# Sixteen experts streamed through one ring of tiles: large and small experts taken by turns

## The chip, the cores and the metric

The kernel runs on one core of one Trainium2 chip. The metric is the device time in microseconds (us) of one execution. Three executions of the kernel before took 1281.28, 1287.78 and 1290.25 us; the median is 1287.78 us.

## The reference: one layer, and most of its bytes are expert weights

The layer has 256 tokens of width 2048 in fp32. A gated short convolution comes first (a projection to 3 x 2048, a depthwise convolution over three tokens, a projection back), modulated by six vectors that come from a conditioning vector times a 2048 x 12288 matrix, then a LayerNorm. The second half is a mixture of 16 experts with top-1 of 4 groups and top-2 of the 4 experts in the group:

```
act = silu(h @ w_gate[e]) * (h @ w_up[e])          # 2048 -> 768, for every expert e
y   = sum over e of (act * combine[:, e]) @ w_down[e]   # 768 -> 2048
x   = layer_norm(ALPHA * x + mod[5] * y)
```

`combine` is zero but for a token's two experts. An expert's weights are 3 x 2048 x 768 x 4 bytes, 18.9 MB, whatever the number of its tokens; the sixteen make 302 MB of the 472 MB that the kernel reads.

## The kernel before, in words

**Ranks and slots.** The kernel counts the tokens of each expert on the chip, sorts the experts by count and calls them by rank. Each rank has a fixed number of slots, `CAPS` (L42): rank 0 is handled apart with 32, ranks 1 to 3 have 128 slots, ranks 4 to 6 have 64, ranks 7 to 15 have 32. A rank with 128 slots is called a large expert here, one with 32 a small one. (What exceeds the slots is done in a loop at the end, L1336, that runs as often as there is excess.)

**The weights.** `expert_loads` (L144) lists 12 tiles of 1.5 MiB for an expert: gate and up weights in turn for four quarters of the 2048 input rows (`q`, four blocks of 128 rows each), then four tiles of down weights. All weights of the kernel go through one list, `loads`, in one order. `get(i)` (L118) asks for tile i, and before it returns it issues the following loads, on SP's queue (SyncE), as far as the ring has room. The ring has `RING = 6` buffers; a load can start when the tile six places earlier in the list has been read for the last time.

**One expert.** `gather` (L892) makes the expert's input in transposed form with one-hot matmuls on TensorE (tiles `gap`), and ScalarE and VectorE modulate it. `run_expert` (L1019) then goes through the quarters. A small expert multiplies its 32 columns with 384-wide pieces of the weights (`gue`, L1049, 128x32 weights in TensorE). A large expert uses 128x128; half of its row blocks go as fp32 (L1049), the others are split on ScalarE (L795) and VectorE (L796) into a high and a low part (`parts`, three pairs of buffers) and multiplied three times (L1045 to L1047). Then come the activation, its transposes (`pte`, L1071) and `down_rows` (L978), which goes through the four down tiles (`dne`; L1007 for a small expert, L1010 to L1012 for a large one). Halfway, at down tile 1, `mid` may call `prepare`, the gather for a later group of experts (`GROUPS`, `PREPARE`, L45). `down_rows` returns a function `finish`, which scales the result (`Y`, L1155) and, for a large expert (`Alone`, L1112) or for the last of a pack of four small ones (`Packed`, L1131), scatters it back to the 256 tokens (`sce`, L1125 and L1163, then an addition into `acc`). It is called after the first quarter of the next expert (`before`, L1051).

**The order of the work.** `SEQ` (L43) gives the ranks in turn, one after the other. Inside this, the framework's own planner sets each engine's order of instructions: it puts work that does not depend on the current expert (the gather, the residual sums `lr`) between its matmuls. Accumulators in PSUM come from six banks (`mm`) and two more (`aux`).

Of the kernel before, what the change touches and what calls it, by code (L numbers as in the profile page):

```python
# [36 lines left out]
AT = 1  # L37
# [28 lines left out]
def trunk_kernel(  # L66
# [77 lines left out]
    def expert_loads(e, pieces=None):  # L144
# [4 lines left out]
        for q in range(4):  # L149
            for src in (ex_w_gate, ex_w_up):  # L150
                def fn(w, src=src, q=q):
                    s = one(src)[:, q * 512 : (q + 1) * 512, :]
                    nc.sync.dma_start(w, s.rearrange("o (p j) f -> p (o j f)", j=4))
                gu.append(add_load(fn))
        if pieces is None:
            for i in range(4):
                def fn(w, hf=i // 2, c0=i % 2 * 3072):
                    s = one(ex_w_down)[:, hf * 384 : hf * 384 + 384, :]
                    nc.sync.dma_start(w, s.rearrange("o (p j) f -> p (o j f)", j=3)[:, c0 : c0 + 3072])
                dn.append(add_load(fn))  # L160
            return gu, dn
        for c0, n in pieces:
            def fn(w, c0=c0, n=n):
                for hf in range(2):
# [4 lines left out]
                    )  # L169
            dn.append((add_load(fn), c0, n))  # L170
        return gu, dn


# [538 lines left out]
    ld_exp = {0: expert_loads(0)}  # L712
    wide["free"] = todo[max(i for i, st in enumerate(steps) if st in last_cin)][0]
# [63 lines left out]
    with tc.tile_pool(name="p2", bufs=1) as p2:  # L777
# [200 lines left out]
        def down_rows(dn, a, al, cc, name, out, mid, at, pieces):  # L978
# [9 lines left out]
            for i, ld in enumerate(dn):  # L988
# [4 lines left out]
                for j, lo_c, hi_c, w0 in rows_:  # L993
                    kt = i // 2 * 3 + j
                    for (c0, n), (bank, off) in zip(pieces, where):
                        f = n // k
                        for g in range(k):
# [20 lines left out]

        def run_expert(lds, xs, cc, name, out, between=(), mid=None, at=0, before=None, pieces=None):  # L1019

# [7 lines left out]
            for q in range(4):  # L1028
                wg, wu = get(gu[2 * q]), get(gu[2 * q + 1])
                for k in range(4):  # L1030
# [3 lines left out]
                    for g in range(4 if cc == 32 else 2):  # L1034
                        for hf in range(1 if cc == 32 else 2):
# [48 lines left out]
            if isinstance(dn[0], int):  # L1084
                return down_rows(dn, a, al if cc == 128 else None, cc, name, out, mid, at, pieces)

# [13 lines left out]
            for i, (ld, c0, n) in enumerate(dn):  # L1100
# [3 lines left out]
                if prev:  # L1104
                    out(*prev)
                prev = (ps, c0, n)
            out(*prev)

        def m5_cols(p0, pn, c0, n):
# [188 lines left out]
        prepare(0)  # L1298
        for r in SEQ[1:]:
            ld_exp[r] = expert_loads(expert_id(r), PIECES if r == SEQ[-1] else None)  # L1300
        done = None
        for r in SEQ:
            if r == SEQ[1]:
                prepare(1)
# [7 lines left out]
            done = run_expert(ld_exp[r], xgs[r], CAPS[r], f"e{r}_", out_r, extra, mid, AT, done,  # L1312
                              PIECES if SEQ[-1] in pack_of.get(r, ()) else None)


# [20 lines left out]
        with tc.For_i(0, nov, 1) as it:  # L1336
# [12 lines left out]
            for h in range(2):  # L1349
# [3 lines left out]
                V.tensor_sub(op_[:, h, :], op_[:, h, :], oc_)  # L1353
            lds = expert_loads(eo)
            xg = gather([(op_, 128)], "ov")
            run_expert(lds, xg, 128, "ov", Alone(op_, ow_, "ov", then=stats2))()
            finish()
# [27 lines left out]
```

## Time and profile before

| | |
|---|---|
| median of three runs | 1287.78 us |
| the profiled execution: its own time, its span | 1292.59 us, 1290.9 us |
| TensorE (PE) busy | 1130.1 us, 88% of the span |
| VectorE (DVE), ScalarE (ACT) busy | 677.3 us (52%), 376.0 us (29%) |
| moved by DMA | 475.60 MB, mean 368 GB/s over the span |
| chain that ended last | PE 62%, DMA 23%, DVE 9%, ACT 2%, issue 2% |

The page also cuts the span into 40 slices of 32.3 us. The experts fill the slices from the 17th on; the rate of the DMA in them reads 340 425 429 429 405 343 322 422 429 406 361 377 428 430 423 337 428 428 429 429 429 429 414 82 GB/s. The busy share of TensorE alone does not say which of the two, matmuls or transfers, ends a stage: a matmul that overlaps others counts as busy, and a transfer that has no free buffer is not waiting by any count.

### The profile page before, as it was taken

Reading aid. Unit: us, or ns where it says so; the run is one execution under the profiler, and the core shown is the slowest. Engines: PE = TensorE matmul, PEld = TensorE weight load, DVE = VectorE, ACT = ScalarE, POOL = GpSimd, SP = SyncE. Lnnn points to the kernel's source line nnn. Section 1 sums busy time; section 2 is a strip of 40 time slices with the busy share of each in tenths; the row PEclk is TensorE's granted clock in tenths of the full one; section 3 lists DMA queues with packets and bytes.
Section 4 is the critical chain, followed back from the end, with each engine's and each line's share of the span. In section 5 each row is a group of like instructions: output and inputs, shape, how many; then the busy total and the mean of one; then the engine's idle time right before and its main releaser. Section 6 shows DMA issues by size and latency. Waiting matters only on the chain.

```text
span 1290.9 us, 19457 instructions
## 1 busy us (share of the span) xinstructions
PE 1130.1 (88%) x7743; PEld 755.7 (59%) x7743; DVE 677.3 (52%) x1273; ACT 376.0 (29%) x662; POOL 9.7 (1%) x50
## 2 busy tenths in 40 slices
PE   4999779999999998976789997999689998789984
PEld 2867659877999964533257543664157443444453
DVE  1456549897999967352255542573146441123127
ACT  1532333533444424140035312451026110100020
POOL 1000000000000000000000000000000000000000
PEclk9999799999999999699889999999899999899996
DMA  9999898689999977899998899999999899999992
GB/s 317 395 400 395 303 382 297 225 312 398 360 334 343 333 280 291 340 425 429 429 405 343 322 422 429 406 361 377 428 430 423 337 428 428 429 429 429 429 414 82
DMA packets 151105, 475.60 MB, mean 368 GB/s; under 512 B 11000, under 2 KB 70104, under 8 KB 126688
## 3 DMA queue, kind: packets, MB, share of 16 engines
q1 hardware_dynamic: 145984, 471.89, 92.6%
q10 hardware_dynamic: 5024, 2.40, 0.7%
q8 instruction: 63, 1.03, 0.3%
q14 instruction: 34, 0.28, 0.1%
HBM read 472.16 MB, written 2.10 MB: 367 GB/s over the span
## 4 chain that ended last, share of the span: by engine, by line
PE 62%; DMA 23%; DVE 9%; ACT 2%; issue 2%; SPq 0%; DVEq 0%; ACTq 0%
DMA w<-in_ex_w_up_dram 19%; PE ci L464 18%; PE gue L1049 14%; PE co L597 6%; DMA w<-in_ex_w_gate_dram 4%; PE dne L1007 3%; PE gap L921 3%; PE gv L269 3%; PE sce L1163 2%; PE gv L299 2%; PE gue L1047 1%; PE dne L1010 1%; PE dne L1011 1%; PE dne L1012 1%; PE gue L1046 1%
## 5 line engine op out<-in xcount | busy, mean ns | idle before, releaser
L1049 PE MATMUL gue<-w,xgp 128*32 128x384 f32 (+1 forms) x1664 | 216.7, 536 | 65.3 <-DMA w<-in_ex_w_up_dram 58.0
L464 PE MATMUL ci<-hhi,hic 128*128 128x256 f32 x768 | 193.2, 289 | 9.0 <-ACT hic L418 7.9
L1049 PEld LDWEIGHTS gue<-w,xgp 128*32 128x32 f32 (+1 forms) x1664 | 80.3, 124 | 197.9 <-issue 88.7
L464 PE MATMUL ci<-hlo,hic 128*128 128x256 f32 x768 | 190.0, 285 | 0.1
L464 PEld LDWEIGHTS ci<-hhi,hic 128*128 128x128 f32 x768 | 148.4, 193 | 18.3 <-ACT hic L418 12.2
L464 PEld LDWEIGHTS ci<-hlo,hic 128*128 128x128 f32 x768 | 148.4, 193 | 0.7 <-DVE hlo L413 0.4
L419 DVE TENSOR_TENSOR loc<-w,hic 128x1024 fp32r<-128x1024 f32 (+1 forms) x108 | 118.5, 1103 | 44.3 <-PE ci L464 22.7
L418 ACT CAST hic<-w 128x1024 fp32r<-128x1024 f32 (+1 forms) x108 | 102.4, 957 | 118.5 <-PE ci L464 71.7
L796 DVE TENSOR_TENSOR parts<-w,parts 128x384 fp32r<-128x384 f32 (+1 forms) x168 | 97.8, 613 | 57.3 <-ACT parts L795 55.3
L464 PE MATMUL ci<-hhi,loc 128*128 128x256 f32 x768 | 110.2, 285 | 7.4 <-DVE loc L419 7.4
L795 ACT CAST parts<-w 128x384 fp32r<-128x384 f32 (+1 forms) x168 | 89.9, 560 | 79.4 <-PE gue L1046 59.9
L464 PEld LDWEIGHTS ci<-hhi,loc 128*128 128x128 f32 x768 | 99.3, 191 | 13.6 <-DVE loc L419 7.6
L1068 ACT COPY gse<-gue 128x384 f32<-128x384 f32 x16 | 7.6, 480 | 313.9 <-PE gue L1049 313.9
L277 DVE SCALAR_TENSOR_TENSOR rows<-w,sT,rows 128x512 f32<-128x512 f32 x105 | 78.2, 749 | 3.6 <-ACT rows L273 2.0
L921 PEld LDWEIGHTS gap<-ohp,xt 128*128 128x128 f32 x512 | 66.2, 209 | 22.6 <-issue 16.0
L921 PE MATMUL gap<-ohp,xt 128*128 128x128 f32 (+2 forms) x512 | 70.4, 294 | 5.7 <-DVE xgp L889 5.0
L1049 PE MATMUL gue<-w,xfp 128*128 128x384 f32 x192 | 71.5, 495 | 1.7 <-DMA w<-in_ex_w_gate_dram 1.7
L1155 DVE TENSOR_TENSOR Y<-dne,m 32x512 f32<-32x512 f32 (+3 forms) x84 | 40.6, 484 | 37.9 <-PE dne L1007 34.6
L889 DVE TENSOR_SCALAR xgp<-gap,GB 128x32 f32<-128x32 f32 (+1 forms) x104 | 31.6, 314 | 48.6 <-ACT xgp L887 48.0
L597 PE MATMUL co<-hio,yh 128*128 128x512 f32 x128 | 52.1, 407 | 1.9 <-DVE t L607 1.4
L887 ACT ACTIVATE xgp<-gap,GB 128x32 f32<-128x32 f32 (+1 forms) x104 | 37.9, 385 | 52.3 <-PE gap L921 29.9
L418 ACT CAST hio<-w 128x1024 fp32r<-128x1024 f32 x32 | 33.2, 1049 | 60.5 <-PE co L597 25.1
(316 smaller groups left out, 1415.4 us busy)
## 6 DMA issues: line engine op xcount, KB each, us to landing
w<-in_ex_w_gate_dram SPq DMA_DIRECT2D x64, 1536.0 KB, 14.6
w<-in_ex_w_up_dram SPq DMA_DIRECT2D x64, 1536.0 KB, 17.1
w<-in_ex_w_down_dram SPq DMA_DIRECT2D x60, 1536.0 KB, 14.0
w<-in_mod_w_dram SPq DMA_DIRECT2D x48, 1536.0 KB, 8.4
w<-in_conv_in_w_dram SPq DMA_DIRECT2D x84, 512.0 KB, 8.3
w<-in_mod_w_dram SPq DMA_DIRECT2D x22, 1024.0 KB, 8.3
w<-in_conv_out_w_dram SPq DMA_DIRECT2D x16, 1024.0 KB, 8.9
w<-in_conv_in_w_dram SPq DMA_DIRECT2D x24, 256.0 KB, 7.2
```

The lines of the kernel that those rows point to most:

```text
L269: TE.matmul(box["ps"][32 * g : 32 * g + 32, :n], sT[:, kt : kt + 1].to_broadcast([P, 32]), ws, start=kt < 4, stop=kt >= 12)
L277: V.scalar_tensor_tensor(out=box["r"][:, :n], in0=ws, scalar=sT[:, kt : kt + 1], in1=box["r"][:, :n], op0=ALU.mult, op1=ALU.add)
L418: S.copy(hi[:, :n], src)
L419: V.tensor_sub(lo[:, :n], src, hi[:, :n].bitcast(F32))
L464: TE.matmul(pss[a][:, b * T : (b + 1) * T], w_[:, o : o + P], h_[:, k0 + k, :], start=first and not low and (b, k, i) == (0, 0, 0), stop=l ...
L597: TE.matmul(pso[h][:, :], y[:, k, h * P : (h + 1) * P], w_[:, k * 512 : (k + 1) * 512], start=not low and (qt % 2, pr, k, i) == (0, 0, 0, ...
L795: S.copy(hi[:, :n], src)
L796: V.tensor_sub(lo[:, :n], src, hi[:, :n].bitcast(F32))
L921: TE.matmul(ps[:, k * n : (k + 1) * n], xn[:, h, (k0 + k) * P : (k0 + k + 1) * P], oh[:, h, :n], start=h == 0, stop=h == 1)
L1007: TE.matmul(ps, a[kt], ws, start=st_, stop=sp_)
L1049: TE.matmul(dst, big[0][:, KF.index(kt), :] if cc == 128 else xg[:, kt, :cc], src, start=st_, stop=sp_)
L1155: V.tensor_tensor(out=y, in0=ps[p0 : p0 + cc, :f], in1=m5_cols(p0, cc, c, f), op=ALU.mult)
```

## The change

The ranks are put into `UNITS`: either one rank, or a large rank with a small one ([1, 14], [2, 12], [3, 10]). `SEQ` is the units one after the other, so each large expert comes one place earlier in it, and its small partner behind it. `queue_loads` enters the loads of a unit into the list by turns: the gate and up tile of a quarter for the first expert, then those of the second, and so on, then the down tiles one of each. `run_expert` and `down_rows` become generators that yield after each quarter and each down tile; `by_turns` steps the generators of a unit in turn and, after the first step, calls what the last unit left (`finish`). `PREPARE` moves the gather of rank 1 from expert 14 to expert 15; the overflow list and the residual sums (`lr`) move from the third to the second expert in `SEQ`, which is 15. No tile, matmul, size or buffer count changes.

```diff
-SEQ = [0, 15, 14, 1, 13, 12, 2, 11, 10, 3, 9, 4, 8, 5, 6, 7]
+UNITS = [[0], [15], [1, 14], [13], [2, 12], [11], [3, 10], [9], [4], [8], [5], [6], [7]]
+SEQ = [r for unit in UNITS for r in unit]
...
-PREPARE = {14: 2, 13: 3, 12: 4, 11: 5, 9: 6, 8: 7}
+PREPARE = {15: 2, 13: 3, 12: 4, 11: 5, 9: 6, 8: 7}
...
+    def queue_loads(fns):
...
+        out = [([], []) for _ in fns]
+        for q in range(4):
+            for (gu, _), (g, _) in zip(fns, out):
+                g += [add(fn) for fn in gu[2 * q : 2 * q + 2]]
+        for i in range(max(len(dn) for _, dn in fns)):
+            for (_, dn), (_, d) in zip(fns, out):
+                d += [add(fn) for fn in dn[i : i + 1]]
+        return out
...
-                if q == 0 and before:
-                    before()
+                yield
...
+        def by_turns(gens, before=()):
+
+            left, live = [], list(gens)
+            while live:
+                for gen in live[:]:
+                    try:
+                        next(gen)
+                    except StopIteration as e:
+                        live.remove(gen)
+                        if e.value:
+                            left.append((-gens.index(gen), e.value))
+                    for fn in before:
+                        fn()
+                    before = ()
+            return [fn for _, fn in sorted(left, key=lambda t: t[0])]
...
-            extra = {SEQ[0]: [sum_m5], SEQ[2]: [overflow_list, residual], SEQ[-1]: [last_rows]}.get(r, [])
+            extra = {SEQ[0]: [sum_m5], SEQ[1]: [overflow_list, residual], SEQ[-1]: [last_rows]}.get(r, [])
...
+        left = []
+        for unit in UNITS:
+            if unit == UNITS[1]:
+                prepare(1)
+            left = by_turns([expert(r) for r in unit], left)
```

Three places show how this moves instructions. The line numbers of the changed kernel are higher by 16 or so.

The first is TensorE's queue at the end of the first quarter of rank 1 (128x384 results are the large expert's, 32x384 a small one's; `w_` is the weight tile that is read). Before:

```order
2324 L1047 MATMUL gue_2_5845<-parts,xhp_5733 128x384
2325 L1045 MATMUL gue_3_5846<-parts,xhp_5733 128x384
2326 L1046 MATMUL gue_3_5846<-parts,xlp_5734 128x384
2327 L1047 MATMUL gue_3_5846<-parts_4884,xhp_5733 128x384
2328 L1049 MATMUL gue_0_5843<-w_5811,xfp_5732 128x384
2329 L1049 MATMUL gue_1_5844<-w_5811,xfp_5732 128x384
```

Now:

```order
2289 L1064 MATMUL gue_3_5717<-parts_4884,xhp_5604 128x384
2290 L1066 MATMUL gue_0_5774<-w_5682,xgp_5322 32x384 x2
2291 L1066 MATMUL gue_0_5774<-w_5690,xgp_5322 32x384 x2
...
2296 L1066 MATMUL gue_0_5774<-w_5682,xgp_5322 32x384 x2
2297 L1066 MATMUL gue_0_5774<-w_5690,xgp_5322 32x384 x2
2298 L1066 MATMUL gue_0_5714<-w_5698,xfp_5603 128x384
2299 L1066 MATMUL gue_1_5715<-w_5698,xfp_5603 128x384
```

A quarter of rank 14, eight rows on its own two tiles, now stands between two quarters of rank 1.

The second is SP's queue at the same unit; `TENSOR_LOAD eid_i` reads the number of the expert whose loads follow. Before:

```order
190 L773 TENSOR_LOAD eid_i
191 L153 ISA
192 L153 DMA w_5619<-in_ex_w_gate_dram 128x3072
193 L153 ISA
194 L153 DMA w_5721<-in_ex_w_up_dram 128x3072
195 L153 ISA
196 L153 DMA w_5811<-in_ex_w_gate_dram 128x3072
```

Now:

```order
165 L789 TENSOR_LOAD eid_i
166 L155 ISA
167 L155 DMA w_5490<-in_ex_w_gate_dram 128x3072
168 L155 ISA
169 L155 DMA w_5592<-in_ex_w_up_dram 128x3072
170 L789 TENSOR_LOAD eid_i
171 L155 ISA
172 L155 DMA w_5682<-in_ex_w_gate_dram 128x3072
173 L155 ISA
174 L155 DMA w_5690<-in_ex_w_up_dram 128x3072
175 L155 ISA
176 L155 DMA w_5698<-in_ex_w_gate_dram 128x3072
```

The second expert's number is read after the first pair of tiles, and from there the tiles of the two alternate in twos.

The third is TensorE's queue around expert 15's down tiles (`lr` is the residual sums, `gap` the gather, `dne` the down product). Before:

```order
2236 L1071 MATMUL pte_0_5511<-ident,gse_0_5509 128x128 x3
2237 L226 MATMUL lr_5652<-T2a,ident 128x128 x3
2238 L1007 MATMUL dne_0_5519<-w_5450,ae__5508 32x512 x6
2239 L226 MATMUL lr_5652<-T2a,ident 128x128
2240 L226 MATMUL lr_5660<-T2a,ident 128x128 x4
2241 L226 MATMUL lr_5667<-T2a,ident 128x128 x4
2242 L1007 MATMUL dne_0_5519<-w_5468,ae__5508 32x512 x6
```

Now:

```order
2246 L1087 MATMUL pte_0_5583<-ident,gse_0_5581 128x128 x3
2247 L937 MATMUL gap_5606<-ohp_5600,xt 128x128 x3
2248 L1023 MATMUL dne_0_5591<-w_5450,ae__5580 32x512 x6
2249 L937 MATMUL gap_5606<-ohp_5600,xt 128x128 x5
2250 L937 MATMUL gap_5625<-ohp_5600,xt 128x128 x8
2251 L1023 MATMUL dne_0_5591<-w_5468,ae__5580 32x512 x2
2252 L937 MATMUL gap_5644<-ohp_5600,xt 128x128 x8
```

The residual sums have moved up between the quarters of expert 15's gate and up product, and the gather for rank 1 has taken their place.

## Rows read from the trace of the kernel before

**Rows 1.** The page: the chain that ended last, its shares by line.

```profile
DMA w<-in_ex_w_up_dram 19%; PE ci L464 18%; PE gue L1049 14%; PE co L597 6%; DMA w<-in_ex_w_gate_dram 4%; PE dne L1007 3%; PE gap L921 3%; PE gv L269 3%; PE sce L1163 2%; PE gv L299 2%; PE gue L1047 1%; PE dne L1010 1%; PE dne L1011 1%; PE dne L1012 1%; PE gue L1046 1%
```

**Rows 2.** Windows (from:to, length, engines busy and counts, clock, DMA share, GB/s).

```profile
548.00:655.00 107.00, 81.01 (x650) 38.95 (x644) 38.99 (x89) 20.39 (x53) 0.00 (x0) 0.94 1.01 428
655.00:760.00 105.00, 97.91 (x529) 62.23 (x522) 57.73 (x130) 39.37 (x84) 0.00 (x0) 0.97 0.90 360
760.00:815.00 55.00, 42.52 (x285) 20.82 (x282) 24.33 (x64) 14.80 (x42) 0.00 (x0) 0.97 1.01 429
815.00:905.00 90.00, 86.54 (x483) 55.56 (x481) 48.91 (x101) 34.99 (x73) 0.00 (x0) 1.00 0.94 377
905.00:980.00 75.00, 57.11 (x313) 32.12 (x314) 22.03 (x51) 14.49 (x31) 0.00 (x0) 0.93 1.01 429
980.00:1045.00 65.00, 61.96 (x376) 35.96 (x374) 38.46 (x79) 26.64 (x58) 0.00 (x0) 1.00 0.93 379
1045.00:1255.00 210.00, 184.32 (x1297) 88.31 (x1300) 41.41 (x97) 20.65 (x47) 3.61 (x2) 0.97 1.01 427
```

**Rows 3.** Waits of TensorE, 548 to 1255 us: total, times, longest.

```profile
PE gue L1049 <- DMA w<-in_ex_w_up_dram: 58.0, 26, 3.1
```

**Rows 4.** Timeline of TensorE, rank 3 alone: start, length, work, idle before.

```profile
947.81 1.56 PE L1049 MATMUL gue<-w,xfp 128*128 128x384 f32 x4 [1.70 <-DMA w<-in_ex_w_gate_dram]
...
985.91 1.21 PE L1071 MATMUL pte<-ident,gse 128*128 128x128 f32 x6
987.02 0.96 PE L1010 MATMUL dne<-parts,ahe 128*128 128x512 f32 x3
...
1004.91 0.83 PE L1049 MATMUL gue<-w,xgp 128*32 128x384 f32 x2
```

**Rows 5.** Timeline of TensorE, gate and up product of small expert 13.

```profile
728.51 2.77 PE L1049 MATMUL gue<-w,xgp 128*32 128x384 f32 x28
...
733.99 6.00 PE L1049 MATMUL gue<-w,xgp 128*32 128x384 f32 x68
742.01 2.77 PE L1049 MATMUL gue<-w,xgp 128*32 128x384 f32 x28 [2.02 <-DMA w<-in_ex_w_up_dram]
```

**Rows 6.** Timeline of TensorE, small expert 9: gather, down product, then its pack's scatter.

```profile
1027.25 0.83 PE L921 MATMUL gap<-ohp,xt 128*128 128x128 f32 x6
1028.04 1.91 PE L1007 MATMUL dne<-w,ae__8048 128*32 128x512 f32 x12
1029.88 3.17 PE L921 MATMUL gap<-ohp,xt 128*128 128x128 f32 x26
1032.98 1.91 PE L1007 MATMUL dne<-w,ae__8048 128*32 128x512 f32 x12
1034.82 3.84 PE L921 MATMUL gap<-ohp,xt 128*128 128x128 f32 x32
1038.59 3.24 PE L1007 MATMUL dne<-w,ae__8048 128*32 128x512 f32 x24
...
1044.99 1.98 PE L1163 MATMUL sce<-Y,st 128*128 128x512 f32 x4
...
1052.50 5.42 PE L1163 MATMUL sce<-Y,st 128*128 128x512 f32 x12
```

**Rows 7.** Timelines of TensorE, then VectorE, at the start of rank 1.

```profile
664.43 0.69 PE L1047 MATMUL gue<-parts,xhp 128*128 128x384 f32 x1 [4.37 <-DVE parts L796]
...
661.00 2.79 DVE L1155 TENSOR_TENSOR Y<-dne,m 32x512 f32<-32x512 f32 x4
```

**Rows 8.** Windows for `gue` alone (PE, PEld, DVE, ACT): expert 14, then rank 1.

```profile
616.00:642.00 26.00, 17.11 (x128) 5.04 (x124) 0.00 (x0) 0.48 (x1) 0.80 1.01 428
658.00:703.00 45.00, 40.41 (x160) 30.31 (x160) 0.55 (x1) 0.98 (x2) 0.92 0.88 352
```

**Rows 9.** Weight tiles, 640 to 760 us: time from issue to landing.

```profile
DMA to landing us min/median/max: 6.1/9.9/19.3
```

**Rows 10.** Instructions of the residual sums on VectorE: ns min/median/max.

```profile
L815 DVE TENSOR_TENSOR acc<-xt,lr x8: 1014/1040/1079, 601.6 to 614.5; 128x512 f32<-128x512 f32 x8
L819 DVE TENSOR_TENSOR acc<-acc,lr x8: 675/680/690, 603.4 to 616.1; 128x512 f32<-128x512 f32 x8
```

More of the change, by code (lines that the diff above doesn't have):

```diff
@@ L153, in fn @@
                     nc.sync.dma_start(w, s.rearrange("o (p j) f -> p (o j f)", j=4))
-                gu.append(add_load(fn))
+                gu.append(fn)
         if pieces is None:
@@ L159, in fn @@
                     nc.sync.dma_start(w, s.rearrange("o (p j) f -> p (o j f)", j=3)[:, c0 : c0 + 3072])
-                dn.append(add_load(fn))
+                dn.append(fn)
             return gu, dn
@@ L169, in fn, with add @@
                     )
-            dn.append((add_load(fn), c0, n))
+            dn.append((fn, c0, n))
         return gu, dn
+    def queue_loads(fns):
+        def add(d):
+            return (add_load(d[0]),) + d[1:] if isinstance(d, tuple) else add_load(d)
+        out = [([], []) for _ in fns]
[6 more added lines that the diff above has]
+        return out
     T1 = const.tile([P, P], F32, name="T1")
@@ L711, in trunk_kernel @@
             dst.append((add_load(load) if load else None, work))
-    ld_exp = {0: expert_loads(0)}
+    ld_exp = {0: queue_loads([expert_loads(0)])[0]}
     wide["free"] = todo[max(i for i, st in enumerate(steps) if st in last_cin)][0]
@@ L1017, in down_rows, with run_expert @@
             return finish
-        def run_expert(lds, xs, cc, name, out, between=(), mid=None, at=0, before=None, pieces=None):
+        def run_expert(lds, xs, cc, name, out, between=(), mid=None, at=0, pieces=None):
             gu, dn = lds
@@ L1050, in run_expert @@
                                           start=st_, stop=sp_)
-                if q == 0 and before:
-                    before()
+                yield
             for fn in between:
@@ L1084, in run_expert @@
             if isinstance(dn[0], int):
-                return down_rows(dn, a, al if cc == 128 else None, cc, name, out, mid, at, pieces)
+                return (yield from down_rows(dn, a, al if cc == 128 else None, cc, name, out, mid, at, pieces))
             def down(ld, c0, n):
@@ L1106, in run_expert @@
                 prev = (ps, c0, n)
+                yield
             out(*prev)
+        def by_turns(gens, before=()):
[12 more added lines that the diff above has]
+            return [fn for _, fn in sorted(left, key=lambda t: t[0])]
         def m5_cols(p0, pn, c0, n):
@@ L1298, in trunk_kernel, with expert @@
         prepare(0)
[L1299 to L1304, printed above, removed]
+        for unit in UNITS[1:]:
+            fns = [expert_loads(expert_id(r), PIECES if r == SEQ[-1] else None) for r in unit]
+            ld_exp.update(zip(unit, queue_loads(fns)))
+        def expert(r):
             then = stats2 if r == SEQ[-1] else None
@@ L1310, in trunk_kernel @@
             mid = (lambda: prepare(PREPARE[r])) if r in PREPARE else None
-            extra = {SEQ[0]: [sum_m5], SEQ[2]: [overflow_list, residual], SEQ[-1]: [last_rows]}.get(r, [])
-            done = run_expert(ld_exp[r], xgs[r], CAPS[r], f"e{r}_", out_r, extra, mid, AT, done,
+            extra = {SEQ[0]: [sum_m5], SEQ[1]: [overflow_list, residual], SEQ[-1]: [last_rows]}.get(r, [])
+            return run_expert(ld_exp[r], xgs[r], CAPS[r], f"e{r}_", out_r, extra, mid, AT,
                               PIECES if SEQ[-1] in pack_of.get(r, ()) else None)
+        left = []
[3 more added lines that the diff above has]
+            left = by_turns([expert(r) for r in unit], left)
         normed = place("normed", 1, [P, 2, D])
@@ L1353, in trunk_kernel @@
                 V.tensor_sub(op_[:, h, :], op_[:, h, :], oc_)
-            lds = expert_loads(eo)
+            lds = queue_loads([expert_loads(eo)])[0]
             xg = gather([(op_, 128)], "ov")
-            run_expert(lds, xg, 128, "ov", Alone(op_, ow_, "ov", then=stats2))()
+            for fn in by_turns([run_expert(lds, xg, 128, "ov", Alone(op_, ow_, "ov", then=stats2))]):
+                fn()
             finish()
```

## The prediction, made before the changed kernel ran

> **What bounds the kernel now.** I read the page's chain of waits first, then the rate of the transfers stretch by stretch, then TensorE's timeline inside the stretches where that rate falls. The chain names weight transfers for 23% (up and gate tiles) and, beside the convolution, the experts' matmuls [rows 1]: neither engine nor transfers bound the whole, so the stages have to be told apart. The reader should see in the windows [rows 2] that the sixteen experts alternate between two states. In 548 to 655, 760 to 815, 905 to 980 and 1045 to 1255 us the transfers run at 427 to 429 GB/s, with a DMA share of 1.01: there the transfers are the bound, and TensorE waits 58.0 us in total for up tiles alone [rows 3]. In 655 to 760, 815 to 905 and 980 to 1045 us they fall to 360, 377 and 379 GB/s while TensorE is busy 93%, 96% and 95% of the time. Those three stretches hold the three large experts: there TensorE is the bound, and the transfers stand still for want of a free buffer.
>
> What stands still can be counted against 429 GB/s: 105 x (429 - 360)/429 = 16.9 us, 90 x 52/429 = 10.9 us, 65 x 50/429 = 7.6 us, together **35.4 us**. This is all that an evener mix of large and small experts can win, since elsewhere in 548 to 1255 us the transfers already run at their rate, and before 548 us nothing is changed.
>
> **What the change does to the balance.** A tile of 1536 KB at 429 GB/s takes 1.573 MB/429 GB/s = 3.67 us, an expert of 12 tiles 44.0 us, a pair of 24 tiles 88.0 us.
>
> *TensorE's work in a pair.* The large expert took 947.81 to 1004.91 us, 57.1 us, in the stretch where it waited for almost nothing [rows 4]; 17.9 us of this is the down product with the small transposes that the planner put in it. The small one needs for its 128 gate and up matmuls 2.77 + 6.00 + 2.77 us for 124 of them [rows 5], about 11.9 us for all; for its down product 1.91 + 1.91 + 3.24 = 7.1 us for 48 [rows 6]; with 0.6 us of transposes (half of the six of rows 4) 19.6 us. Together **76.7 us against 88.0 us of transfers**: 11.3 us to spare in each pair. Alone, the large expert's 57.1 us stands against 44.0 us; of those 13.1 us too many, the ring of six tiles hides a part and the rest is lost.
>
> *What else falls into a pair.* [2, 12] also has the gather of ranks 11 to 8, which hangs on expert 12: 0.83 + 3.17 + 3.84 = 7.8 us [rows 6]; and the scatter of the pack that ends with 13, which the next unit calls: 1.98 + 5.42 = 7.4 us [rows 6]. So 76.7 + 15.2 = 91.9 us, 3.9 us over the transfers; the ring (six tiles, 22 us of transfers) lies between, so this becomes a late end of the pair rather than a standstill, and expert 11 behind it needs only 19.6 + 7.8 (its gather of rank 3) + 7.4 (rank 2's scatter, of the same eight 128x512 products as rows 6) = 34.8 us for its 44.0. The other two pairs carry no gather.
>
> *The start of a pair.* Rank 1 began with a wait of 4.37 us, since VectorE had `Y` (2.79 us) and the pack's tables ahead of the first `parts` [rows 7], and its gate and up product went from 658 to 703 us at a granted clock of 0.92 [rows 8], 45 us against the 38.1 us of rank 3 (947.81 to 985.91) at a clock of 1.00 [rows 4, 2]. In the new order VectorE has the same tables and the same `Y`, now of expert 15, ahead of the first `parts`. I take these 6.9 us over: 83.6 us for pair [1, 14], still 4.4 us under 88.0.
>
> *The buffers.* A large quarter holds its two tiles for 38.1/4 = 9.5 us, and no load can follow into them meanwhile. Alone, two tiles (7.3 us of transfers) are freed every 9.5 us. In the pair, four tiles (14.7 us) are freed every 9.5 + 3.0 = 12.5 us, so the ring keeps filled; but for 9.5 us in a row nothing comes free, and a load needs at least 6.1 us from issue to landing [rows 9], 2.4 us more than its share of the rate. The trace does not show such a mix. Its bounds: nothing is lost (gain 35.4), or each pair still loses as much as rank 3 does alone, 3 x 7.6 = 22.8 us (gain 12.6). I take 3 us for [1, 14] with its late start, 3 us for [2, 12] with its 3.9 us too many and 1 us for [3, 10], 7 us in all: nearer to nothing, as the 11.3 us to spare come from measured rows.
>
> *Expert 15.* It gets the residual sums and the gather of rank 1; expert 14 loses them. TensorE: 7.8 us each. The residual sums' sixteen VectorE steps, 8 x 1.040 + 8 x 0.680 = 13.8 us [rows 10], now stand between expert 15's gate and up quarters, which are spread over the 29 us of their eight tiles and hold only 11.9 us of matmuls. The gather takes the place that it had in expert 14's down stage. 19.6 + 7.8 + 7.8 = 35.2 us for 44.0 us: covered. Without this cover it would cost at most the 13.8 us.
>
> *SP, VectorE, ScalarE, PSUM.* SP issues the same loads; the second read of an expert's number now stands between the first two and the next two tiles of a pair, when four earlier tiles are still on their way, so nothing. VectorE was busy 57.7 of 105 us around rank 1 [rows 2], and a small expert adds almost none. A pair holds four PSUM banks and one, and its down products four and one, of six: the scatter in [2, 12]'s first quarter has two banks instead of four to alternate between, which I count in the 3 us.
>
> **The sum.** 35.4 - 7 = 28.4 us less: 1292.6 (the profiled execution's own time; span 1290.9) becomes 1264.2. That execution lies 4.8 us over the median of the runs, 1287.8, so for a median I expect 1287.8 - 28.4 = **1259 us**. The tail after 1255 us and everything before 548 us stay.
>
> **The rivals.**
>
> *The pairs lose half of it still.* The 9.5 us in which nothing comes free starve the transfers in every quarter, and each pair loses what rank 3 loses now: gain 12.6 us, **1275 us**. For it: in the stretch of rank 3, transfers fell to 379 GB/s though it began with an almost empty TensorE queue. Against: only two tiles per 9.5 us came free there, not four per 12.5.
>
> *No gain.* The experts behind the pairs would have to take the time back, by being bound by TensorE. For it: TensorE is busy 184.3 of 210 us in 1045 to 1255 us. Against: the transfers run at 427 GB/s there, so a start that is 28 us earlier ends 28 us earlier. Another way to the same time: the transfers have no room. Neighbouring stretches show 428 and 429 GB/s [rows 2], so there is room for 19% over the 360. The Trainium skill, "DMA: Bandwidth & Descriptors", section Specifications, gives about 358 GB/s as the HBM's limit for one core; by that rule the large experts' stretches would already be at the ceiling, the pairs would win nothing and the time would be 1288 us. Rows 2 speak against the rule in this case. Time **1288 us**. That the planner undoes the turns is out: the queues in the section on the change show them.
>
> *Slower: TensorE at its lower clock in the pairs.* TensorE now works in blocks of 9.5 and 3.0 us with short waits between, and where it waited for tiles between blocks, in expert 14's gate and up product, the granted clock was 0.80 of full [rows 8], part of the time at 1.2 instead of 2.4 GHz. The gate and up products of a pair are 38.1 + 11.9 = 50 us at full clock; if a share f of them ran at half clock, a pair would need 76.7 + 50 f us. The transfers cover 11.3 of it; each pair would then lose 50 f - 11.3 us, as much as now (35.4/3 = 11.8) from f = 0.46 on. With f = 1 the three lose 116 us: 1287.8 + 116 - 35.4 = 1368; with f = 0.75, 79 us: **1331 us**. Against: rank 3, which is fed without waits, had a clock of 1.00, and a pair waits 11 us in 88, not 9 in 26 as expert 14 did. The Trainium skill, "TensorE: Matmul & The Clock Gate", section on HAM oscillation, describes just this, a clock that falls in each wait for a tile. By that rule the small blocks between waits would run slow; the trace agrees for the small experts alone, and no row shows it for a mix.
>
> **How the numbers follow.** The forecast has 0.69, and in its own range the loss in the pairs is 0 to 16 us: 1252 to 1268. Half a loss has 0.14 (1268 to 1281), no gain 0.10, slower 0.07. The range takes the first two, with 4 us below for the scatter of the runs (1281.3 to 1290.3): **1248 to 1281**; 0.17 is left out. One per cent, about what a measurement of this kernel can tell from no change, is 12.9 us, that is 1274.9. Faster by more than that: 0.69 and half of the 0.14, 0.76. Within it: the other half and the 0.10, 0.17. Slower: 0.07.
>
> **What would show it.** In the changed profile the three pairs should run at 415 GB/s or more, with TensorE waiting for tiles here and there inside them, and the last expert should end some 28 us earlier, with the same tail. A pair at 380 to 400 GB/s with TensorE busy throughout is the first rival; a rate of 429 in the pairs and a lower one behind them the second; a granted clock under 0.8 in the pairs the third. The forecast is wrong if a pair's matmuls take more than 88 us.

## The result, and the profile after

The changed kernel took 1270.07 us (median of four runs, 1266.35 to 1272.44), the kernel before 1289.01 us (four runs, 1281.28 to 1290.60): a ratio of 0.9868, 95% interval 0.9839 to 0.9897. It is 18.9 us faster. That lies in the range, on the side that was forecast, but the gain is two thirds of the 28.4 us that the sum gave.

The windows of the changed kernel, cut near its own stages (expert 0 and the start of 15; 15's gate and up product; its down product; [1, 14]; 13 and the first large quarter of [2, 12]; the rest of [2, 12]; 11; [3, 10]; the rest), answer to [rows 2]:

```profile
543.00:571.00 28.00, 21.51 (x187) 11.83 (x180) 15.24 (x39) 12.40 (x32) 0.00 (x0) 1.00 1.01 424
571.00:595.00 24.00, 19.06 (x150) 11.24 (x153) 14.16 (x21) 1.52 (x5) 0.00 (x0) 0.86 0.77 301
595.00:616.00 21.00, 20.38 (x162) 11.23 (x154) 9.76 (x38) 7.02 (x18) 0.00 (x0) 1.00 1.00 424
616.00:703.00 87.00, 80.11 (x423) 50.18 (x421) 41.17 (x83) 32.51 (x67) 0.00 (x0) 0.96 1.01 424
703.00:760.00 57.00, 48.62 (x295) 23.05 (x294) 23.15 (x51) 9.59 (x24) 0.00 (x0) 0.94 1.01 429
760.00:849.00 89.00, 85.95 (x463) 53.42 (x465) 47.94 (x105) 39.23 (x92) 0.00 (x0) 0.98 0.96 403
849.00:885.00 36.00, 33.48 (x255) 15.81 (x247) 15.60 (x37) 5.48 (x14) 0.00 (x0) 1.00 0.99 397
885.00:970.00 85.00, 78.46 (x415) 48.08 (x411) 40.87 (x93) 31.83 (x68) 0.00 (x0) 0.96 1.01 428
970.00:1231.00 261.00, 228.96 (x1548) 107.67 (x1550) 63.45 (x140) 28.91 (x71) 3.62 (x2) 0.95 1.01 428
```

The last number of each row is to be read first. Two of the three pairs run at 424 and 428 GB/s, where a large expert alone ran at 360 and 379 [rows 2]. But expert 15 (301 GB/s) and expert 11 (397), which were full before, are not now, and [2, 12] reaches only 403 (rank 2 alone: 377). Counted against 429 GB/s as in the prediction: 24 x 128/429 = 7.2 us at expert 15, 1.0 us in [1, 14], 5.4 us in [2, 12], 2.7 us in expert 11, 0.2 us in [3, 10], 1.1 us in the other rows; together 17.6 us. Before, the same sum was 36.6 us (35.4 us and 1.2 us in the stretches at 427 and 428). So 19.0 us fewer are lost, and 18.9 us is what the medians show.

The profiled executions themselves differ by more, 1292.59 against 1268.98 us. 5.0 us of that come from ahead of the change: the first expert's first gate matmul stands at 542.39 us before and at 537.44 us after. From there to the end of the span it is 748.5 us before and 729.8 us after, 18.7 us less.

TensorE's waits from 540 to 1255 us answer to [rows 3] (total, times, longest):

```profile
PE gue L1066 <- DMA w<-in_ex_w_up_dram: 32.0, 14, 2.8
...
PE lr L242 <- DVE acc L831: 4.9, 3, 2.4
...
PE lr L242 <- DVE xgp L905: 2.5, 1, 2.5
```

Waiting for up tiles fell from 58.0 to 32.0 us; the residual products (`lr`) waited 7.4 us for VectorE. In the page's chain TensorE's share rose from 62% to 66%, and that of DMA fell from 23% to 16%.

**The standstill at expert 15.** TensorE's timeline there (start, length, work, count, and in brackets the idle time before it with its releaser):

```profile
567.18 0.84 PE L1066 MATMUL gue<-w,xgp 128*32 128x384 f32 x4
570.52 1.13 PE L242 MATMUL lr<-T2a,ident 112*128 112x128 f32 x8 [2.50 <-DVE xgp L905]
574.01 2.04 PE L242 MATMUL lr<-T2a,ident 112*128 112x128 f32 x8 [2.36 <-DVE acc L831]
575.99 4.11 PE L1066 MATMUL gue<-w,xgp 128*32 128x384 f32 x28
580.02 2.05 PE L242 MATMUL lr<-T2a,ident 112*128 112x128 f32 x16
583.33 0.46 PE L242 MATMUL lr<-T2a,ident 112*128 112x128 f32 x2 [1.25 <-DVE acc L831]
583.72 0.84 PE L1066 MATMUL gue<-w,xgp 128*32 128x384 f32 x4
584.49 1.83 PE L242 MATMUL lr<-T2a,ident 112*128 112x128 f32 x14
587.57 2.10 PE L242 MATMUL lr<-T2a,ident 112*128 112x128 f32 x14 [1.26 <-DVE acc L831]
589.60 2.77 PE L1066 MATMUL gue<-w,xgp 128*32 128x384 f32 x28
```

And the loads that SP issued in the same stretch:

```profile
565.76 0.33 SPq L155 DMA_DIRECT2D w<-in_ex_w_up_dram  x1
579.52 0.33 SPq L155 DMA_DIRECT2D w<-in_ex_w_gate_dram  x1
...
591.80 4.64 SPq L161 DMA_DIRECT2D w<-in_ex_w_down_dram  x4
```

Each quarter's 32 `gue` matmuls are torn apart: 4 of them, then residual sums that wait for VectorE, then the 28 that read the tiles for the last time (575.99 to 580.1, 589.60 to 592.4 us). Loads go out as these end, from 579.52 and from 591.80 us, and none in the 13.8 and 11.7 us before. Six tiles are 22 us of transfers; two such pauses in a row, 25.5 us with two tiles in between, empty the ring.

**The losses in and behind [2, 12].** There are two, of about equal size: 2.7 us in the pair's first quarter (16 x 73/429), and 4.7 us at its end and in expert 11:

```profile
763.44:779.44 16.00, 16.00 (x74) 8.16 (x75) 8.28 (x14) 2.36 (x5) 0.00 (x0) 1.00 0.88 356
835.44:867.44 32.00, 30.36 (x176) 12.92 (x175) 20.89 (x43) 9.15 (x22) 0.00 (x0) 1.00 0.93 366
```

TensorE and SP in the first quarter:

```profile
761.47 7.60 PE L1196 MATMUL sce<-Y,st 128*128 128x512 f32 x16
769.00 2.79 PE L1066 MATMUL gue<-w,xgp 128*32 128x384 f32 x32
```

```profile
761.04 0.33 SPq L155 DMA_DIRECT2D w<-in_ex_w_up_dram  x1
771.82 0.33 SPq L155 DMA_DIRECT2D w<-in_ex_w_gate_dram  x1
```

The scatter of the pack that ends with 13 takes 7.60 us, as long as priced (7.4), but it stands between the large expert's first quarter and the small one's, so the small one's two tiles are held behind it and no load goes out for 10.8 us. That pause is not enough by itself: e8, below, has the same scatter in the same place and the same pause, and loses nothing there. What differs is how much was still on its way when the pause began.

### The profile page after: what moved, and what is told of

Read it like the earlier page. It is cut to its first block, busy times and chain, and to the rows that moved or that the text cites. A ratio compares the mean times of both kernels' runs of the same rounds, so it can differ in the third digit from the quotient of the medians.

```text
span 1267.2 us, 19443 instructions
## 1 busy us (share of the span) xinstructions
PE 1132.6 (89%) x7743; PEld 752.4 (59%) x7743; DVE 676.7 (53%) x1273; ACT 374.0 (30%) x662; POOL 9.8 (1%) x50
## 4 chain that ended last, share of the span: by engine, by line
PE 66%; DMA 16%; DVE 11%; ACT 3%; issue 2%; DVEq 0%; SPq 0%; ACTq 0%
PE ci L480 18%; PE gue L1066 16%; DMA w<-in_ex_w_up_dram 12%; PE co L613 6%; PE gap L937 4%; PE dne L1023 4%; PE sce L1196 3%; PE gv L285 3%; DMA w<-in_ex_w_down_dram 2%; DVE Y L1188 2%; PE gv L315 2%; PE gue L1064 1%; DVE rows L293 1%; DVE loc L435 1%; PE gue L1063 1%
## 5 line engine op out<-in xcount | busy, mean ns | idle before, releaser
L1066 PE MATMUL gue<-w,xgp 128*32 128x384 f32 (+1 forms) x1664 | 208.5, 527 | 34.2 <-DMA w<-in_ex_w_up_dram 32.0
L1066 PE MATMUL gue<-w,xfp 128*128 128x384 f32 x192 | 74.2, 512 | 0.0
L905 DVE TENSOR_SCALAR xgp<-gap,GB 128x32 f32<-128x32 f32 (+1 forms) x104 | 31.8, 314 | 46.2 <-ACT xgp L903 45.6
## 6 DMA issues: line engine op xcount, KB each, us to landing
w<-in_ex_w_up_dram SPq DMA_DIRECT2D x64, 1536.0 KB, 16.5
```

## The experiments

All ratios are against the kernel before on the same chip, with a 95% interval. Beside them stand two numbers from each profile: the **stage**, from the first expert's first gate matmul to the end of the span, and the **lost transfers** in it, summed over windows of 8 us against 429.5 GB/s up to where the last loads run out. A sum from one profile is uncertain by some 3 us: the two profiles of the changed kernel differ by 2.6 us.

| run | ratio [interval] | stage, us | lost, us | stage - lost |
|---|---|---|---|---|
| before | 1 | 748.5 | 36.6 | 711.9 |
| changed | 0.9868 [0.9839, 0.9897] | 729.8 | 17.7 | 712.1 |
| changed, again (e9) | 0.9843 [0.9812, 0.9873] | 728.9 | 15.1 | 713.8 |
| e1 | 1.0083 [1.0051, 1.0114] | 758.7 | 47.1 | 711.6 |
| e2 | 0.9834 [0.9804, 0.9864] | 727.2 | 17.0 | 710.2 |
| e3 | 0.9915 [0.9889, 0.9941] | 737.3 | 21.8 | 715.5 |
| e4 | 0.9966 [0.9950, 0.9981] | 744.0 | 31.8 | 712.2 |
| e5 | 0.9838 [0.9816, 0.9861] | 728.6 | 17.5 | 711.1 |
| e6 | 0.9886 [0.9865, 0.9906] | 734.2 | 20.0 | 714.2 |
| e7 | 0.9831 [0.9805, 0.9857] | 724.4 | 9.9 | 714.5 |
| e8 | 0.9876 [0.9852, 0.9900] | 731.6 | 16.6 | 715.0 |
| e10 | 0.9779 [0.9755, 0.9803] | 721.4 | 10.1 | 711.3 |
| e11 | **0.9759 [0.9735, 0.9783]** | 719.1 | 8.1 | 711.0 |
| e12 | 0.9794 [0.9768, 0.9820] | 724.8 | 12.0 | 712.8 |

Whatever the order, the stage takes 710 to 716 us and its lost transfers. That is mostly bookkeeping: the runs load the same weights, so a stage is these bytes at the full rate, the lost transfers, and a start and a tail without loads. That the column stays so even shows that the full rate and the tail hardly moved; it does not show what loses the transfers. e3, e6, e7 and e8, at 714 to 716, have a longer tail (e10 tells why).

**The move to expert 15, alone, in the old order (e1).**

```diff
-extra = {SEQ[0]: [sum_m5], SEQ[2]: [overflow_list, residual], ...
+extra = {SEQ[0]: [sum_m5], SEQ[1]: [overflow_list, residual], ...
```

> The kernel before, experts one after the other, with one line changed: the residual sums and the overflow list are emitted at expert 15 instead of 14. In TensorE's queue the residual products then stand between the first two quarters of expert 15, as they do in the changed kernel. Theory (held tiles): the residual products wait for VectorE's sums, 13.8 us in all, and behind them in the queue stand the matmuls that would free expert 15's first tiles; the transfers fall to 160 GB/s for some 8 us and the kernel is 6 to 8 us slower than the kernel before, ratio 1.005 to 1.006. Rival (the pairs themselves lose the missing gain, and the hole at expert 15 is only where the ring shows it): TensorE's work is the same, so the time is that of the kernel before within 2 us, ratio 0.998 to 1.002.

Measured 1296.86 us against 1285.92: 10.9 us slower, from one line. Its windows at expert 15:

```profile
567.00:591.00 24.00, 19.06 (x148) 11.35 (x151) 14.38 (x23) 1.75 (x5) 0.00 (x0) 0.86 0.75 297
```

It is the row 571 to 595 us of the changed kernel over again (301 GB/s, TensorE 19.06 us busy), without any pair. Lost transfers rise from 36.6 to 47.1 us, the size of the slowdown, but only 7.3 us of this stand at expert 15, near the 6 to 8 us expected. Most of the rest is in rank 2's stretch, which loses 13.5 us here and 10.2 us in the profile of the kernel before; the line changes nothing there, and e4 loses the same 13.5 us. So the hole at 15 belongs to the move, not to the turns; the other 3 us have no cause that a run shows.

**Taking it away again in the new order (e2, e5).** e2 puts the same work at the pair's small expert, 14 (`SEQ[1]` becomes `SEQ[3]`).

> The changed kernel with one line changed: the residual sums and the overflow list are emitted at expert 14, so that the residual products stand at the end of the first pair's gate and up work and in its down product, and expert 15's quarters are free of them. Theory (held tiles at expert 15): the hole of 7 us at expert 15 closes, the pair has 11 us of TensorE to spare for 8 us of products, and the time falls by 4 to 7 us against the changed kernel: ratio to the kernel before 0.981 to 0.984. Rival (the pairs lose it): the loss reappears in pair 1, ratio 0.986 to 0.988 as in the changed kernel.

e5 leaves out the matmuls that broadcast two rows of the LayerNorm for the residual (`lr`), so those two rows are missing from its result, and keeps VectorE's steps:

```diff
-ps = aux_tile(f"lr0{i}{q}")
-row_bcast(ps, T2a, 112, r0 + q * 4)
...
-V.tensor_add(o, o, ps[:, :])
+V.tensor_add(o, o, xn[:, h, q * 512 : (q + 1) * 512])
```

> The changed kernel without the 32 residual products on TensorE: VectorE's sixteen steps of the residual sums stay, with another operand, so this leaves the two LayerNorm rows of the residual out of the result. Theory (held tiles): the hole at expert 15 (7 us) is made by these products standing in TensorE's queue ahead of the matmuls that free its tiles; without them it closes and the kernel is 6 to 8 us faster than the changed kernel, ratio to the kernel before 0.980 to 0.983. Rival (it was VectorE's 13.8 us, or the pair behind, that made the loss): ratio 0.985 to 0.988, as the changed kernel.

e2 took 1265.30 us (0.9834) and e5 1265.93 us (0.9838), ratios that overlap those of the changed kernel. The profiles say why. In e2, expert 15 first, then places where loss reappeared, in pair [1, 14] and, after 710 us, in expert 13:

```profile
572.00:596.00 24.00, 13.27 (x107) 3.89 (x100) 2.90 (x10) 2.54 (x7) 0.00 (x0) 0.93 1.01 430
616.00:632.00 16.00, 14.07 (x73) 9.24 (x74) 6.54 (x13) 3.90 (x8) 0.00 (x0) 0.89 0.96 390
680.00:696.00 16.00, 13.72 (x85) 8.97 (x84) 11.31 (x18) 3.11 (x7) 0.00 (x0) 1.00 0.91 365
700.00:732.00 32.00, 29.70 (x196) 12.49 (x194) 15.69 (x25) 4.24 (x7) 0.00 (x0) 1.00 0.96 394
```

The hole at 15 is gone (430 GB/s), and 1.5, 2.4 and 2.6 us come back behind it. In e5 TensorE waits for tiles at expert 15 again, as a transfer-bound stretch should:

```profile
556.25 5.35 PE L1021 MATMUL dne<-w,ae__5269 128*32 128x512 f32 x24 [7.12 <-DVE ae__5269 L1096]
...
581.22 2.77 PE L1064 MATMUL gue<-w,xgp 128*32 128x384 f32 x28 [1.02 <-DMA w<-in_ex_w_up_dram]
```

Its loss at 15 falls from 7.3 to 2.8 us, but it grows from 2.7 to 4.5 us in the first quarter of [2, 12], and the total is 17.5. The 2.8 us most likely have a cause of their own: VectorE's steps, which no longer wait for products, now run ahead of expert 0's activation, and TensorE waits 7.12 us for that (the first row), in a stretch without a load from 546.73 to 559.91 us. So the products make the hole, but filling it alone gains little: e2's total is 0.7 us less than the changed kernel's and 1.9 us more than that of its second profile (e9, 15.1). How much of the 7.3 us comes back by that alone is not settled.

**One pair alone (e4):** only [3, 10], the residual sums and the gathers of rank 1 where they were.

```diff
-UNITS = [[0], [15], [1, 14], [13], [2, 12], [11], [3, 10], ...
+UNITS = [[0], [15], [14], [1], [13], [12], [2], [11], [3, 10], ...
```

> Only [3, 10] is taken by turns; all other experts run alone, in the order and with the gathers and residual sums of the kernel before. The large rank 3 cost 7.6 us of transfers alone. Theory (turns win the whole of it when nothing else falls into the pair): 6 to 8 us faster than the kernel before, ratio 0.994 to 0.9955, with 427 GB/s or more through the pair. Rival (a pair keeps half of its loss): 3 to 4 us, ratio 0.997 to 0.998.

1280.77 us against 1285.92, 5.2 us less. The interval touches both expectations, so the ratio alone decides nothing; the profile does. The loss of rank 3, 7.3 us before by the 8-us windows, is down to 92 x 4/429 = 0.9 us in this stretch; the total falls by only 4.8 us, as rank 2's stretch loses 3.3 us more than in the profile before (see e1):

```profile
880.00:972.00 92.00, 84.44 (x497) 52.52 (x498) 43.19 (x108) 32.84 (x73) 0.00 (x0) 0.98 1.01 425
```

Turns do what they were costed to do in this pair, where nothing else lies in it.

**Partners from the other side (e3, e6, e7).** e3 pairs each large expert with the small one that used to follow it, which leaves 15 and 14 alone and puts the residual sums back at 14:

```diff
+UNITS = [[0], [15], [14], [1, 13], [12], [2, 11], [10], [3, 9], [4], [8], [5], [6], [7]]
+PREPARE = {14: 2, 13: 4, 12: 3, 10: 5, 9: 6, 8: 7}
+XG = [1, 0, 0, 0, 1, 0, 0, 1]
```

> The same turns with other partners: [1, 13], [2, 11] and [3, 9], so that expert 14 stays a small expert alone ahead of the first pair, the residual sums stay where they were before the change, and the pack that ends with 13 is scattered in expert 12's turn, a small expert alone, not between the first quarters of a large and a small one; the gather of ranks 11 to 8 moves to pair [1, 13] with another buffer. Theory (the shortfall is expert 15's hole, 7 us, and what falls into pair [2, 12], 8 us): at least 10 of these 15 us come back, ratio to the kernel before 0.977 to 0.980. Rival (the pairs lose it): every pair still loses some 5 us, ratio 0.985 to 0.988.

This did not come: 1274.12 us, 0.9915. The pairs and expert 15 are full, and two new holes have opened, at experts 12 and 4:

```profile
538.00:748.00 210.00, 176.80 (x1178) 98.61 (x1174) 97.39 (x227) 64.32 (x156) 0.00 (x0) 0.97 1.01 427
748.00:768.00 20.00, 20.00 (x128) 7.86 (x124) 10.03 (x16) 0.00 (x0) 0.00 (x0) 1.00 0.71 267
768.00:1026.00 258.00, 237.06 (x1353) 138.28 (x1346) 118.69 (x261) 83.92 (x184) 0.00 (x0) 0.98 1.01 428
1026.00:1042.00 16.00, 16.00 (x54) 6.15 (x54) 9.17 (x14) 0.00 (x0) 1.80 (x1) 1.00 0.34 144
```

TensorE at the second hole:

```profile
1022.84 5.80 PE L1196 MATMUL sce<-Y,st 128*128 128x512 f32 x12
1028.56 5.61 PE L1158 MATMUL sce<-m,sTe__7521 128*128 128x512 f32 x12
1034.10 1.50 PE L1066 MATMUL gue<-w,xgp 128*64 128x384 f32 x4
```

A pair now leaves two scatters at once, its pack's and the large expert's, and both stand in a block ahead of the next expert's second quarter; between 1022.94 and 1041.62 us SP issues no load. TensorE is busy throughout (16.00 of 16.00): nothing waits, and the transfers still stop.

e6 is e3 with the scatters spread, one after each quarter:

```diff
-for fn in before:
+for fn in before[:1]:
     fn()
-before = ()
+before = before[1:]
```

> The kernel with the partners [1, 13], [2, 11], [3, 9], and one line more: the two scatters that a pair leaves are called one after the first and one after the second step of the next unit, not both after the first. The amount of work is the same. Theory (scatters in one block of 15 us between the first and the second quarter of experts 12 and 4 hold their tiles and starve the ring): the two holes of 7 and 12 us shrink to less than half, the time falls by 9 to 15 us against that kernel, ratio to the kernel before 0.980 to 0.984. Rival (too much TensorE work in that unit, wherever it stands): 0.989 to 0.993 as before.

e7 is e6 with expert 8 (32 slots) ahead of expert 4 (64 slots), so that the small one stands behind the last pair.

> The same, and the small expert 8 comes ahead of expert 4, so that both scatters behind pair [3, 9] fall into a unit of 32 slots with 20 us of own TensorE work and not into one of 64 with over 30. Theory: the hole at expert 4 closes but for 1 us, all the transfers from the first expert on lose under 5 us; ratio to the kernel before 0.974 to 0.979. Rival (the amount in the whole stage decides, not where it stands): no better than the kernel with 4 first, within 2 us.

e6 took 1273.02 us (0.9886), mostly a miss: the hole at 12 shrank from 7.4 to 4.5 us, that at 4 only from 11.7 to 11.1. e7 took 1265.22 us (0.9831), and that hole fell to 2.1 us; the whole stage lost 9.9 us, not under 5, and the ratio is outside both expectations. Spreading helped little behind expert 4 with its 64 slots; with the small expert 8 there, most of the hole went.

**The gather out of [2, 12] (e8):** moved into expert 14's half of the first pair, with its buffer.

```diff
-PREPARE = {15: 2, 13: 3, 12: 4, 11: 5, 9: 6, 8: 7}
+PREPARE = {15: 2, 14: 4, 13: 3, 11: 5, 9: 6, 8: 7}
+XG = [1, 0, 0, 0, 1, 0, 0, 1]
```

> The changed kernel with the gather of ranks 11 to 8 moved from pair [2, 12] to pair [1, 14] (another buffer for its result); pair [2, 12] then has only the scatter of the pack besides its own work. Theory (8 us of gather behind 7 us of scatter make pair [2, 12] end late, 4.9 us of transfers lost around its end; a gather alone has room in a pair): 4 to 5 us faster than the changed kernel, ratio to the kernel before 0.982 to 0.984. Rival (a gather costs a pair the same wherever it is): no difference from the changed kernel, 0.985 to 0.988.

1270.88 us, 0.9876: no gain, as the rival had it. The hole went with the gather, from the second pair to the end of the first and the expert behind it:

```profile
690.00:732.00 42.00, 39.75 (x227) 19.73 (x229) 25.62 (x54) 14.90 (x35) 0.00 (x0) 0.98 0.90 368
740.00:890.00 150.00, 139.29 (x798) 76.65 (x796) 72.74 (x163) 44.76 (x98) 0.00 (x0) 0.98 1.01 429
```

But the loss in [2, 12]'s first quarter is gone as well, although the scatter still stands there. TensorE's 7.60 us of it begin at 764.79 us, SP pauses for the same 10.8 us, and the transfers run on (SP's loads before and behind the pause, then two windows):

```profile
764.36 0.33 SPq L155 DMA_DIRECT2D w<-in_ex_w_up_dram  x1
775.13 0.33 SPq L155 DMA_DIRECT2D w<-in_ex_w_gate_dram  x1
763.46:771.46 8.00, 8.00 (x24) 3.58 (x23) 4.69 (x7) 1.20 (x3) 0.00 (x0) 1.00 1.03 438
771.46:779.46 8.00, 8.00 (x52) 4.13 (x51) 3.73 (x7) 1.34 (x3) 0.00 (x0) 1.00 0.99 422
```

The load that SP issued just ahead of the pause (here at 764.36 us, in the changed kernel at 761.04 us) tells how much was queued. From issue to landing, first in the changed kernel, then in e8:

```profile
DMA to landing us min/median/max: 11.6/11.6/11.6
DMA to landing us min/median/max: 15.1/15.1/15.1
```

With 15.1 us of transfers on their way the pause of 10.8 us costs nothing; with 11.6 us it costs 2.7 us, since the next load needs some microseconds to land (6.7 us for the one at 771.82 us). Five profiles have this pair with this pause: with 11.6, 11.7 (e9) and 11.8 us (e5) queued they lose 2.7, 2.0 and 4.5 us in its first quarter, with 14.0 us (e2) 1.0 us, with 15.1 us (e8) nothing. The order is not perfect (e5), so the landing of one load is a rough measure. In e8 that load lands 6.8 us later than in the changed kernel while the scatter starts only 3.3 us later: the hole in the pair before delayed the transfers by more than TensorE, and so covers this pause.

The last runs share one chip with the changed kernel (e9), whose 1268.34 us they are to be set against.

> The changed kernel itself, so that the variants beside it are compared on one chip. Both theories: ratio to the kernel before 0.984 to 0.989, as measured.

It gave 0.9843 [0.9812, 0.9873], beside 0.9868 at first; its holes are the same ones (7.2 us at expert 15; 2.0 us and 3.3 us in and behind [2, 12]).

**The tail (e10)** is e7 with the buffers of the last two row tiles exchanged, since in e3, e6, e7 and e8 the first of them shared a buffer with the last expert's input:

```diff
-tag="xg1" if r0 == KT else "xg0"
+tag="xg0" if r0 == KT else "xg1"
```

> The kernel with the partners [1, 13], [2, 11], [3, 9], spread scatters and expert 8 ahead of 4, in which the two last LayerNorm rows change places between two buffers: with the gathers in other buffers the first of them had waited for the last expert's gate and up product, which drew the tail out by about 3 us. Theory: the tail is that of the changed kernel again, 2 to 4 us less than with the buffers as they were, ratio to the kernel before 0.978 to 0.982, 5 to 10 us less than the changed kernel on the same chip. Rival (the amount of work in the stage decides): ratio as the changed kernel's within 2 us.

1262.03 us, 0.9779, 6.3 us less than the changed kernel on the same chip. The last column of the table falls from 714.5 to 711.3 us: the 3 us of the tail are back. The ratio fell by more than that (from 0.9831, on another chip); the rest I can't assign.

**The fastest run (e11)** is e10 with the gather of ranks 11 to 8 in expert 15. The planner then puts the residual products between the quarters of expert 14; in e10 they stood in 15's down product:

```diff
-PREPARE = {14: 2, 13: 4, 12: 3, 10: 5, 9: 6, 8: 7}
+PREPARE = {15: 4, 14: 2, 12: 3, 10: 5, 9: 6, 8: 7}
-extra = {..., SEQ[2]: [overflow_list, residual], ...
+extra = {..., SEQ[1]: [overflow_list], SEQ[2]: [residual], ...
```

> The same with the gather of ranks 11 to 8 moved from pair [1, 13] to expert 15; the planner then puts the residual products between the first quarters of expert 14, as they stood between those of 15 in the changed kernel. Theory (held tiles): a hole of 5 to 7 us opens at expert 14 where none was, the end of pair [1, 13] and expert 12 lose 3 to 4 us less; in sum 1 to 4 us slower than the last one, ratio 0.980 to 0.985. Rival (only the amount counts, and it has gone to a lone small expert with room): no hole, 3 to 4 us faster, 0.975 to 0.979.

1257.98 us, 0.9759: 10.4 us less than the changed kernel on the same chip, 32.2 us less than before, and 4.1 us less than e10, whose interval overlaps. So the theory of held tiles missed here: it had 1 to 4 us slower, and the ratio is the rival's. Its windows (expert 15 and the start of 14; 14's quarters with the residual products; the rest of 14 and the gate and up product of [1, 13]; the rest of that pair and expert 12; [2, 11], 10 and [3, 9]; expert 8):

```profile
542.00:618.00 76.00, 55.59 (x448) 28.72 (x441) 32.84 (x89) 25.93 (x71) 0.00 (x0) 0.95 1.01 426
618.00:634.00 16.00, 14.74 (x136) 8.29 (x135) 9.42 (x12) 0.00 (x0) 0.00 (x0) 0.92 0.87 337
634.00:710.00 76.00, 70.55 (x435) 44.03 (x431) 32.28 (x82) 23.96 (x55) 0.00 (x0) 1.00 1.01 426
710.00:796.00 86.00, 79.84 (x453) 40.09 (x445) 46.79 (x94) 25.08 (x54) 0.00 (x0) 1.00 1.01 429
796.00:1024.00 228.00, 209.15 (x1188) 122.10 (x1187) 105.63 (x223) 74.37 (x161) 0.00 (x0) 0.98 1.01 426
1024.00:1048.00 24.00, 23.38 (x213) 12.12 (x212) 8.93 (x16) 2.10 (x6) 1.80 (x1) 1.00 1.00 408
```

The residual products still cost 16 x 92/429 = 3.4 us where they now stand. So a hole did open, as the theory had it and the rival did not, but half as large as the 5 to 7 us expected: SP's pauses there are 12.9 and 8.3 us, against 13.8 and 11.7 at expert 15 of the changed kernel. The 4.1 us that e10 loses at expert 12 are gone (429 GB/s). 337 GB/s is the only rate under 400 in these rows; 8.1 us are lost in all.

**Both gathers in 14 (e12)** is e10 with 14 making two gathers (`PREPARE = {14: [2, 4], ...}`).

> The same with that gather moved to expert 14 beside the gather of rank 1; the residual products stay in expert 15's down product, and half of the moved gather stands in the first quarter of rank 1. Theory: no hole at 14 or 15; rank 1's first two tiles are held some 4 us longer, the end of the pair and expert 12 lose 3 us less: 0 to 4 us faster than with the gather in pair [1, 13], ratio 0.975 to 0.981, the fastest of all.

1262.58 us, 0.9794: inside the expected ratio, but not the fastest and no better than e10. What it saved behind [1, 13] it lost as 3.9 us in rank 1's first quarter.

## Why the prediction was right in sign and too large in size

**The pairs themselves: right.** The step on the balance (76.7 us of matmuls against 88.0 us of transfers) and the step on the buffers both held: TensorE was busy 80.1 of 87 us in [1, 14] and 78.5 of 85 us in [3, 10]. [1, 14] was given 3 us of retained loss and has 1.0; [3, 10] was given 1 and has 0.2, and e4 shows that pair's gain with no other pair.

**Expert 15: the step that failed.** "19.6 + 7.8 + 7.8 = 35.2 us for 44.0 us: covered" was costed at nothing; it lost 7.2 us. The work came to some 40 us, more than the sum but still under 44.0 (gate and up 13.9, `lr` 10.0, gather 8, down product and transposes 8.4); its order was not looked at. The `lr` matmuls wait for VectorE's sums, and the `gue` matmuls that would free the tiles stand behind them in TensorE's queue. The third piece of the order ahead of the prediction says that the sums now stand between expert 15's quarters, so this could have been seen. Without its cover the prediction had "at most the 13.8 us", and the 7.2 us are inside that. e1 isolates the move: the same hole, 7.3 us, and a kernel that is 10.9 us slower.

**[2, 12]: mis-sized.** The 15.2 us of side work (gather 7.8, scatter 7.4) were found, and 3 us taken for them, as "a late end of the pair rather than a standstill". 8.1 us came, and at 403 GB/s the pair missed the 415 that the prediction named as its sign: 5.4 us in the pair and 2.7 us in expert 11, which was to make up for it. The late end was there, with about 2.5 us in the pair and the 2.7 us behind it; so was a standstill at the start, 2.7 us, which the prediction had ruled out. The scatter's own 7.60 us were right; its place ahead of the small expert's reads was left out, and so was that the ring is not always six tiles ahead: 11.6 us were queued when the pause of 10.8 us began, not 22. e8 shows both at once: without the gather in the pair the late end is gone, and with 15.1 us queued the same pause costs nothing.

**The sum.** 7 us were taken; 7.2 + 1.0 + 5.4 + 2.7 + 0.2 = 16.5 us came. 28.4 - (16.5 - 7) = 18.9 us, the difference of the medians. That it fits to the tenth is luck: the interval of the ratio leaves 13 to 21 us, and the second profile of the same kernel lost 2.6 us less. The starting point, that only lost transfers can be won, held: the table's last column hardly moves.

**The rivals.** By its number the result belongs to the first rival: 1270 us lies in the 1268 to 1281 us that the prediction gave to half a loss with 0.14, not in the forecast's own 1252 to 1268. But half the loss did not remain as that rival had it: it put the loss into every quarter of every pair, 22.8 us in the three, where 6.6 us came. That the two agree in size is chance. No gain is out. The Trainium skill, "DMA: Bandwidth & Descriptors", section Specifications, has a limit of about 358 GB/s for one core. It does not bind here: 85 us of [3, 10] ran at 428 GB/s. The slower clock is out as well: the pairs' rows show 0.96, 0.98 and 0.96 of full clock, against 0.75 of the matmuls at half clock that the rival needed for its 1331 us.

**What stays open.** The holes are not independent. From 571 to 885 us TensorE of the changed kernel is busy 287.6 of 314 us (the rows above), so a hole that is closed there brings the next tight place sooner; that is how I read e2, e5 and e8. The five profiles of [2, 12] bear it out for one pause, but no run changes how much is queued and nothing else.

## What to carry to other kernels

Where a ring of buffers feeds an engine with an in-order queue, adding up the engine's work per stage is not enough: ask of each piece of side work which buffer-freeing reads stand behind it, and how long that block is against the transfers still queued when it begins, which can be much less than the whole ring. Side work that waits for another engine, or comes as one block, belongs into a stage with spare time. Giving each lone small expert one kind of it made the fastest run here, though the theory had expected otherwise. Count the lost transfers of the whole stage after each edit, since one closed hole can open the next.

## What the runs showed of the hardware beyond that

The transfers of one core held 426 to 429 GB/s over stretches of 76 to 228 us (e11) while TensorE was 73% to 93% busy: with the busier TensorE the rate was no lower (426 GB/s at 73%, 429 at 93%). A busy TensorE and a starved DMA can go together: 16.00 us busy of 16.00 at 144 GB/s (e3). What a pause in the issue of loads costs depends on what is queued: 10.8 us cost 2.7 us of transfers with 11.6 us queued (changed kernel), and nothing with 15.1 us (e8). And code ahead of the first expert's gate matmul, which no kernel here changed, ended between 532.87 and 542.39 us in the fourteen profiles; that scatter alone is as large as some of the effects, and is why the stage was measured from that matmul on.
